# An mLSTM and RG-LRU trunk: the order of the row mask and the score weights, and the PSUM tile of a head's last chunk

## The chip, the cores and the metric

The kernel runs on one core of a Trainium2 chip. The metric is the device time of one execution in microseconds; the median of a few executions is compared. A profile is one further execution, with its own time. Engines go by their short names in the profile: PE is TensorE (matmuls), PEld its weight loads, DVE is VectorE, ACT is ScalarE, POOL is GpSimd, SP is SyncE, which here only issues DMAs.

## The reference

A two-layer decoder trunk over 2048 tokens of width 1024 in float32: an mLSTM layer, then an RG-LRU layer, each behind an RMSNorm and with a residual, and a final RMSNorm. The change concerns the middle of the mLSTM layer. Per head (4 heads, key width 256, value width 512) and chunk of tokens it computes

```python
D = F[..., :, None] - F[..., None, :] + ib[..., None, :]
D = jnp.where(causal, D, -jnp.inf)
m_t = jnp.maximum(F + m[..., None], jnp.max(D, axis=-1))
W = jnp.exp(D - m_t[..., None])
Sm = jnp.einsum('bhtk,bhsk->bhts', qb, kb) * W
num = decay[..., None] * (q C) + (Sm v);  den = decay * (q n) + sum(Sm)
hb = num / jnp.maximum(jnp.abs(den), jnp.exp(-m_t))[..., None]
C_new = d_last * C + (w_last k)^T v
```

(the einsums of `num` and `C_new` are shortened). Then `hh = o * hb` is normed over the head's 512 values to `(hh - mu) * rsqrt(var + EPS)`, scaled by `norm_w`, and `y = (hn + skip * xc) * silu(z)` goes to the output projection.

## The kernel before, in words

There are four phases: the input projections and the gate scans (a1), the mLSTM recurrence (`phase_a2`), the output projection with the second layer's input projection (b1), and the RG-LRU itself with its output (b2). Large products are split in a high and a low float32r part, three matmuls for one (lines 391 to 393); `split_into` (lines 806 and 809) makes the parts: ScalarE casts the high one, VectorE subtracts for the low one.

`phase_a2` works on 4 heads of 8 blocks, a block being 256 tokens or two chunks of 128, so a head has chunks `ch` 0 to 15. It is a software pipeline: in the loop step of block i stand block i's recurrence and block i+1's projections. In the order of the program, one step holds:

- `norm` of block i-1 (line 1144): ScalarE turns the gated `hh` to its norm with the scale and bias in `frs`.
- `loads` of block i+1: SP loads `qb` (line 918, the stabilizer of each token, broadcast over partitions), `db`, `xc`, `xm`, `sz`, `o`; the input splits `xch`, `xcl`, `xmh`, `xml`.
- `recur` of the block's first chunk: the state update `kv` (then line 1090 on VectorE, and the state's parts `Ch` and `Cl`), and the numerator `n` (scores times values, and query times the old state). Lines 1112 to 1122 divide `n` and gate it to `hh`; lines 1131 and 1132 take its mean and variance `mv`.
- `finish` of block i-1: TensorE transposes `hh` to `pt` (line 1157), ScalarE takes it out as `y` (line 1161), VectorE adds and multiplies (1163, 1164), GpSimd stores it (1166).
- `qk` of block i+1: GpSimd masks `qb` with an affine select (line 968: tokens behind the row's own get 3.0e38, so that their weight becomes 0), ScalarE makes the row weights `wgt = exp(gT - qb)` in two halves (line 974), TensorE the query and key projections, taken out as `qT` (995) and `kT` (1005); skip terms `skx`.
- `recur` of the second chunk; at its end GpSimd makes the block's `frs` in four small instructions (lines 1137 to 1140), the second of which in program order is the power -0.5.
- `score` (line 1026; VectorE multiplies by `wgt` at 1028; transposed keys `kh`, `kl`), then the value projections, taken out as `vh` and `vl`.

Besides, parts of the next head's q and k weights and of the second layer's weights are loaded, split and stored in between (`wraw`; 768 wide for the gate weights, 1024 wide for the rest), and in a head's first block the value weights `vwh`, `vwl`.

Each engine runs its instructions in a fixed order, set at build time: a scheduler goes through the program by priority and a cost model, and puts an instruction where its operands and buffers are ready by that model. `self.order(first, then)` adds a constraint: on one engine, `then` stands behind `first`; it makes no wait on another engine. Buffers are rings: `qb` and `wgt` have two each, so the mask of block j can only be loaded when the weights of block j-2 are made. PSUM has eight banks: four for tag "r" (projections, scores, transposes), two for one `kv` tile (pool `pk`), two for one `n` tile (pool `p1`). The profile's line numbers are those of this listing.

Of the kernel before, what the change touches and what calls it, by code (L numbers as in the profile page):

```python
# [7 lines left out]
F32 = mybir.dt.float32  # L8
# [6 lines left out]
P = 128  # L15
# [322 lines left out]
class Trunk:  # L338
# [481 lines left out]
    def phase_a2(self, wq, wk, wv, rgate, rwout, D, late):  # L820
# [3 lines left out]
        with ExitStack() as ctx:  # L824
# [9 lines left out]
            pk = ctx.enter_context(tc.tile_pool(name="psK", bufs=1, space=PSUM, reuse_waits="tile"))  # L834
            p1 = ctx.enter_context(tc.tile_pool(name="psS", bufs=1, space=PSUM, reuse_waits="tile"))
# [10 lines left out]
            nc.gpsimd.memset(mh, -0.5)  # L846
            halves = lambda t: t.rearrange("p (a b) -> p a b", a=2)[:, :, 0:256]
            VA = (slice(0, 258), slice(258, 516))
            self.ygated = ()
            W = {}  # L850

            def head_weights(h, names):
# [54 lines left out]
            def project(h, b):  # L907
# [58 lines left out]
                def qk():  # L966
                    qb = S["qb"]
                    selected = nc.gpsimd.affine_select(qb, qb, pattern=[[0, 2], [1, P]], compare_op=ALU.is_ge, fill=3.0e38,
                                                       base=0, channel_multiplier=-1)
                    if h and b == 1:  # L970
                        self.order(self.rooted, (selected,))
                    wgt = lx.tile([P, 2, P], F32, tag="wgt", name="wgt")
                    for c in range(2):
                        a = nc.scalar.activation(wgt[:, c], qb[:, c], AF.Exp, bias=self.gT[:, r0 + c:r0 + c + 1],
                                                 scale=-1.0)
                        if (h, b) == (0, 1):
                            self.order((self.kT,), (a,))
                        if (h, b) == (0, 2):
                            self.order(self.valued, (a,))
                        if (h, b) == (0, 0):  # L980
                            self.order(self.tail[-1:], (a,))
                            self.first = S.setdefault("w", ()) + (a,)
                            S["w"] = self.first
                    S["wgt"] = wgt
                    xh, xl = S["xc"]
                    for nm in ("q", "k"):
                        wh, wl = W[h][nm]
                        ps = pr.tile([P, 2, BL], F32, tag="r", name="pj")
                        for m in range(2):
                            for k in range(KV):  # L990
                                ms = slice(m * P, (m + 1) * P)
                                self.mm3(ps[:, m], wh[:, k, ms], wl[:, k, ms], xh[:, k], xl[:, k], k == 0, k == KV - 1)
                        t = lx.tile([P, 2, BL], F32, tag=nm + "T", name=nm + "T")
                        if nm == "q":
                            self.qT = nc.scalar.activation(t, ps, AF.Copy, scale=DK ** -0.5)
                            qd = sp.tile([P, 2, BL], F32, tag="qd", name="qd", bufs=2)
                            nc.vector.scalar_tensor_tensor(qd, ps, DK ** -0.5,
                                                           S["db"].unsqueeze(1).to_broadcast([P, 2, BL]),
                                                           op0=ALU.mult, op1=ALU.mult)
                            qh = dp.tile([P, 2, BL], F32R, tag="qh", name="qh")  # L1000
                            ql = dp.tile([P, 2, BL], F32R, tag="ql", name="ql")
                            self.qsplit = self.split_into(qh, ql, qd, "a", "v")
                            S["qd"] = (qh, ql)
                        else:
                            self.kT = nc.scalar.copy(t, ps)
                            if (h, b) == (0, 0):
                                self.order((self.kT,), self.first + self.qsplit)
                        S[nm + "T"] = t
                    if b == 0:
                        head_weights(h, ("v0", "v1"))  # L1010
                    end = (h, b) == final
                    S["skx"] = skx = (late if end else lp).tile([P, KV, BL], F32, tag="kwh" if end else "skx", name="skx")
                    for k in range(KV):
                        a = nc.scalar.activation(skx[:, k], S["xcf"][:, k], AF.Copy, scale=self.v("sk", h * KV + k))
                        if (h, b) != (0, 0):
                            self.order(self.state[:1], (a,))
                        else:
                            self.skips = (self.skips if k else ()) + (a,)
# [27 lines left out]
                def value(c):  # L1046
# [11 lines left out]
                    if (h, b, c) == (0, 0, 1):  # L1058
                        self.order(self.valued, self.skips)

                return S, [loads, qk, score, lambda: value(0), lambda: value(1)]

            C = {}

            def recur(h, b, c, S):
                ch = b * 2 + c
# [1 line left out]
                cs = slice(c * P, (c + 1) * P)  # L1068
                i = ch % NVA
                sh, sl = (t[:, c] for t in S["sm"])  # L1070
                pn = p1.tile([P, 2, 512], F32, tag="n", name="n")
                outs = tuple(pn[:, a, 0:258] for a in range(2))

                def within():
# [101 lines left out]
            for i, (h, b) in enumerate(blocks):  # L1176
                if i + 1 < len(blocks):
                    Sn, (loads, qk, score, v0, v1) = project(*blocks[i + 1])
                else:
                    Sn, loads = None, lambda: None  # L1180
                    qk = score = v0 = v1 = loads
                if last:
                    norm(*last)
                loads()
                extra = b < 5 if h == H - 1 else 2 <= b <= 6
                if extra:
                    next(later, None)
                recur(h, b, 0, S)
                if last:
                    finish(*last)  # L1190
                qk()
                recur(h, b, 1, S)
                score()
                v0()
                if extra and b == 6:
                    next(later, None)
                v1()
                if extra and b < 6:
                    next(later, None)
                if b < 2 and h < H - 1:  # L1200
                    head_weights(h + 1, "qk"[b])
                last = (h, b, S)
                S = Sn
# [746 lines left out]
```

## Time and profile before

Three executions took 2874.71, 2876.73 and 2876.86 us, a median of 2876.73. The profiled execution took 2875.3 us.

| what | value |
|---|---|
| profiled execution's own time | 2875.3 us |
| its span, first to last instruction | 2873.5 us |
| mean granted TensorE clock | 0.996 |
| TensorE busy, 0 to 1000 us (a1 and the start of a2) | 973.4 us |
| TensorE busy, 1000 to 1678.8 us (a2) | 653.7 of 678.8 us |
| TensorE busy, 1678.8 us to the end (b1, b2) | 1177.7 of 1194.7 us |
| VectorE, ScalarE, GpSimd busy in a2 | 571.6, 446.0, 120.5 us |
| DMA share of the 16 engines in a2 | 0.59 |

How to read it. A row of the waits gives engine and line, what ended the wait, the total in us, how many times, and the longest. A row of the busy times by stretch gives the stretch, its length, then PE, PEld, DVE, ACT and POOL busy with the number of instructions, the granted clock, the DMA share and GB/s. A row of the timeline gives start, length, engine, line, operation, names and shapes, and in brackets the engine's idle time before it with what ended it. Instructions of one engine overlap a little, so an idle stretch is counted from the modelled end of the one before.

### The profile page before, as it was taken

The page shows a single profiled execution, that of the slowest core. Times are in us where ns is not written, and L with a number is a line of the kernel's source. Part 1 is how long each engine was busy: PE and PEld are TensorE (multiplying, and loading weights), DVE is VectorE, ACT ScalarE, POOL GpSimd, SP SyncE. Part 2 cuts the span into 40 slices and gives each one's busy share as a digit, 9 for nine tenths or more (in the row PEclk, how much of TensorE's full clock was granted, in tenths as well). Part 3 has the DMA queues.
Part 4 walks back from the last instruction along what each step waited for, and adds up shares of the span by engine and source line. Part 5 has one row for each costly group of instructions (what it writes and reads, how often), then busy time and mean ns, then how long its engine had stood idle before and what let it go on. Part 6 is the DMA issues. An engine that isn't in the chain of part 4 may idle for free.

```text
span 2873.5 us, 43332 instructions
## 1 busy us (share of the span) xinstructions
PE 2804.8 (98%) x15442; PEld 2427.9 (84%) x15442; DVE 2132.4 (74%) x3657; ACT 1515.8 (53%) x2577; POOL 456.1 (16%) x846
## 2 busy tenths in 40 slices
PE   7999999999999999999999999999999999999998
PEld 5799987889987899998989988888788888788886
DVE  7766789635668688888888876768989658777774
ACT  6444455523444466666666653434444423977771
POOL 1211123101212211112121121101221111000000
PEclk9999999999999999999999999999999999999999
DMA  6766777668998755556575568876776765898866
GB/s 233 271 216 225 244 250 267 205 211 268 319 314 271 260 185 192 191 180 206 166 229 192 196 250 274 307 234 209 260 253 224 241 203 178 308 317 306 290 221 205
DMA packets 292472, 687.38 MB, mean 239 GB/s; under 512 B 29088, under 2 KB 103584, under 8 KB 292256
## 3 DMA queue, kind: packets, MB, share of 16 engines
q1 hardware_dynamic: 225072, 451.13, 49.1%
q0 software_dynamic: 66608, 232.43, 21.3%
q8 instruction: 122, 2.00, 0.3%
q10 hardware_dynamic: 576, 1.05, 0.1%
q14 instruction: 94, 0.77, 0.1%
HBM read 447.32 MB, written 237.17 MB: 238 GB/s over the span
## 4 chain that ended last, share of the span: by engine, by line
PE 41%; issue 4%; DVE 3%; ACT 2%; DMA 1%; POOL 1%; POOLq 0%; DVEq 0%; ACTq 0%; SPq 0%
PE pc L391 2%; PE pc L393 2%; PE pc L392 2%; PE pd L392 2%; PE pd L393 2%; PE pd L391 2%; PE pa L391 2%; PE acc L392 2%; PE pa L393 2%; PE acc L393 2%; PE pa L392 2%; PE acc L391 2%; PE pj L391 1%; PE pj L392 1%; PE pj L393 1%
## 5 line engine op out<-in xcount | busy, mean ns | idle before, releaser
L806 ACT CAST s<-raw 128x512 fp32r<-128x512 f32 (+1 forms) x280 | 172.6, 620 | 259.5 <-PE pd L393 72.7
L809 DVE TENSOR_TENSOR s<-raw,s 128x512 fp32r<-128x512 f32 (+1 forms) x280 | 192.1, 689 | 54.1 <-ACT s L806 53.1
L391 PE MATMUL acc<-yh,wr 128*128 128x512 f32 x384 | 148.5, 391 | 2.4 <-ACT R L1671 1.1
L392 PE MATMUL acc<-yl,wr 128*128 128x512 f32 x384 | 149.9, 390 | 0.2 <-DVE yl L809 0.2
L393 PE MATMUL acc<-yh,wr 128*128 128x512 f32 x384 | 149.4, 389 | 0.0
L806 ACT CAST u<-t 128x512 fp32r<-128x512 f32 x112 | 69.1, 620 | 151.8 <-PE pc L393 49.4
L732 DVE SCALAR_TENSOR_TENSOR xc<-xm,vec,xc 128x512 f32<-128x512 f32 x192 | 139.4, 747 | 5.6 <-ACT xc L731 4.9
L809 DVE TENSOR_TENSOR u<-t,u 128x512 fp32r<-128x512 f32 x112 | 77.1, 689 | 76.3 <-ACT u L806 76.3
L806 ACT CAST s<-sum 128x512 fp32r<-128x512 f32 (+1 forms) x120 | 74.1, 618 | 110.2 <-PE pc L393 39.2
L391 PE MATMUL pa<-u,s 128*128 128x512 f32 x304 | 119.1, 392 | 0.3 <-ACT y L1161 0.3
L393 PE MATMUL pa<-u,s 128*128 128x512 f32 x304 | 118.6, 390 | 0.0
L392 PE MATMUL pa<-u,s 128*128 128x512 f32 x304 | 118.5, 390 | 0.0
L1090 DVE SCALAR_TENSOR_TENSOR C<-C,dl,kv 128x516 f32<-128x516 f32 x112 | 83.8, 749 | 45.0 <-PE kv L393 45.0
L732 DVE SCALAR_TENSOR_TENSOR xc<-xr,vec,xc 128x512 f32<-128x512 f32 x144 | 105.9, 747 | 8.9 <-ACT xc L731 7.8
L806 ACT CAST Ch<-C 128x516 fp32r<-128x516 f32 x120 | 72.7, 623 | 67.8 <-DVE da L1112 53.8
L391 PE MATMUL pj<-vwh,xmh 128*128 128x512 f32 x256 | 102.8, 402 | 0.0
L393 PE MATMUL pj<-vwh,xml 128*128 128x512 f32 x256 | 100.0, 391 | 0.0
L392 PE MATMUL pj<-vwl,xmh 128*128 128x512 f32 x256 | 99.8, 390 | 0.0
L809 DVE TENSOR_TENSOR s<-sum,s 128x512 fp32r<-128x512 f32 (+1 forms) x120 | 82.4, 688 | 21.4 <-ACT s L806 20.5
L1144 ACT ACTIVATE hh<-hh,frs 128x512 f32<-128x512 f32 x64 | 51.6, 814 | 88.3 <-POOL frs L1140 88.3
L391 PEld LDWEIGHTS acc<-yh,wr 128*128 128x128 f32 x384 | 71.9, 188 | 19.5 <-DMA wr<-d_ow 1.7
L391 PE MATMUL pd<-u,s 128*128 128x512 f32 x224 | 87.1, 389 | 0.0
(501 smaller groups left out, 10055.9 us busy)
## 6 DMA issues: line engine op xcount, KB each, us to landing
wr<-d_ow SPq DMA_DIRECT2D x96, 512.0 KB, 4.4
d_wx<-s POOLq DMA_DIRECT2D x64, 512.0 KB, 4.4
s<-d_wx SPq DMA_DIRECT2D x64, 512.0 KB, 4.7
s<-d_ws SPq DMA_DIRECT2D x64, 512.0 KB, 6.3
raw<-in_wxz_dram SPq DMA_DIRECT2D x124, 256.0 KB, 4.7
d_wr<-s POOLq DMA_DIRECT2D x48, 512.0 KB, 3.8
s<-d_wr SPq DMA_DIRECT2D x48, 512.0 KB, 4.5
raw<-in_rwin_dram SPq DMA_DIRECT2D x94, 256.0 KB, 4.2
```

The source lines that it names most:

```text
L391: mm(out, sh, mh, start=first, stop=False, skip_group_check=resumed)
L392: mm(out, sh, ml, start=False, stop=False, skip_group_check=resumed)
L393: mm(out, sl, mh, start=False, stop=last, skip_group_check=resumed)
L732: self.convd = [nc.vector.scalar_tensor_tensor(out, x[:, j:j + TB], self.v(wn, m * 4 + j), out, op0=ALU.mult, op1=ALU.add) for j in range( ...
L806: a = nc.scalar.copy(hi, src)
L809: b = (nc.gpsimd if lo_eng == "p" else nc.vector).tensor_tensor(lo, src, hi.bitcast(F32), op=ALU.subtract)
L1090: v = nc.vector.scalar_tensor_tensor(C2, C2, self.dl[:, r:r + 1], p2, op0=ALU.mult, op1=ALU.add)
L1144: return [nc.scalar.activation(hn, hn, AF.Identity, bias=rs[:, 1, c:c + 1], scale=rs[:, 0, c:c + 1]) for c, hn in enumerate(S["hh"])]
```

## The change

Three edits in `phase_a2`:

1. The mask of every block is ordered behind the last of the four instructions that made the latest `frs` (`self.rooted`, empty at first). Before, this held only for the second block of heads 1 to 3.
2. The two halves of a block's `wgt` are ordered behind that block's `kT` on ScalarE, from block 3 of head 0 on.
3. The numerator `n` of a head's last chunk (`ch == 15`, which has no state update) is put in the `kv` tile instead of the `n` tile.

```diff
-            self.ygated = ()
+            self.ygated = self.rooted = ()
...
-                    if h and b == 1:
-                        self.order(self.rooted, (selected,))
+                    self.order(self.rooted, (selected,))
...
+                        weighted = (weighted if c else ()) + (a,)
...
                             self.kT = nc.scalar.copy(t, ps)
+                            if h or b > 2:
+                                self.order((self.kT,), weighted)
...
-                pn = p1.tile([P, 2, 512], F32, tag="n", name="n")
+                pn = (pk if ch == 15 else p1).tile([P, 2, 512], F32, tag="kv" if ch == 15 else "n", name="n")
```

No instruction is added or taken away. Two lines are new ahead of some of the code, so that line 1137 of before is line 1139 of the change, and so on. The orders of TensorE and VectorE stay as they were but for the first block of a head; those of ScalarE, GpSimd and SP change in nearly every block.

GpSimd in a middle block of head 0, before: the mask of a block further on, the four instructions of `frs`, two stores of weights, the store of `y`.

```order
L968 AFFINE_SELECT qb<-qb 128x256
L1137 TENSOR_SCALAR frs<-mv 128x2
L1139 TENSOR_SCALAR frs<-mv 128x2
L1138 TENSOR_TENSOR frs<-frs,mh 128x2
L1140 TENSOR_TENSOR frs<-frs 128x2
L904 DMA d_gw<-wraw 128x768 x2
L1166 DMA d_y<-y 128x4x256
```

The same place in the change:

```order
L1139 TENSOR_SCALAR frs<-mv 128x2
L1141 TENSOR_SCALAR frs<-mv 128x2
L1140 TENSOR_TENSOR frs<-frs,mh 128x2
L1142 TENSOR_TENSOR frs<-frs 128x2
L968 AFFINE_SELECT qb<-qb 128x256
L904 DMA d_gw<-wraw 128x768 x2
L1168 DMA d_y<-y 128x4x256
```

The mask went from the front of the powers to behind them. Before, 18 blocks had a mask directly in front and others none, since the masks ran up to five blocks ahead; in the change there is one behind each block's powers: behind those of block j stands the mask of block j+2.

ScalarE from `kT` on, in a middle block of head 1, before:

```order
L1005 COPY kT<-pj 128x512
L806 CAST xch<-xc 128x1024
L806 CAST Ch_12502<-C_12369 128x516
L806 CAST Ch_12526<-C_12388 128x516
L806 CAST sh<-sm 128x256
L1041 ACTIVATE kh<-kt,wlT 128x256
L974 ACTIVATE wgt<-qb,gT 128x128 x2
L1055 CAST vh_9962<-pj 128x2x256
L1041 ACTIVATE kh<-kt,wlT 128x256
L1144 ACTIVATE hh<-hh,frs 128x512
```

and in the change:

```order
L1005 COPY kT<-pj 128x512
L973 ACTIVATE wgt<-qb,gT 128x128 x2
L806 CAST xch<-xc 128x1024
L806 CAST Ch_12502<-C_12369 128x516
L806 CAST Ch_12526<-C_12388 128x516
L806 CAST sh<-sm 128x256
L1043 ACTIVATE kh<-kt,wlT 128x256
L1057 CAST vh_9962<-pj 128x2x256
L1043 ACTIVATE kh<-kt,wlT 128x256
L1146 ACTIVATE hh<-hh,frs 128x512
```

The two halves of `wgt` went from behind the first `kh` to behind `kT`. They are also those of another block now: of the block whose `kT` stands there.

VectorE at the start of head 2, from the query's low part on, before:

```order
L809 TENSOR_TENSOR ql<-qd,qh 128x512
L809 TENSOR_TENSOR vwl<-wraw,vwh 128x1024 x2
L1112 TENSOR_SCALAR da<-n 128x1
L1028 TENSOR_TENSOR sm<-s,wgt 128x256
L1113 SCALAR_TENSOR_TENSOR da<-n,da,enT 128x1
L1042 SCALAR_TENSOR_TENSOR kl<-kt,wlT,kh 128x256
L1115 RECIPROCAL da<-da 128x1
L809 TENSOR_TENSOR sl<-sm,sh 128x256
L1122 SCALAR_TENSOR_TENSOR hh<-n,da,o 128x512
L1042 SCALAR_TENSOR_TENSOR kl<-kt,wlT,kh 128x256
L1131 BN_STATS st<-hh 128x6
L1056 TENSOR_TENSOR vl_9964<-pj,vh_9960 128x2x256
```

and in the change:

```order
L809 TENSOR_TENSOR ql<-qd,qh 128x512
L1114 TENSOR_SCALAR da<-n 128x1
L1115 SCALAR_TENSOR_TENSOR da<-n,da,enT 128x1
L809 TENSOR_TENSOR vwl<-wraw,vwh 128x1024 x2
L1117 RECIPROCAL da<-da 128x1
L1030 TENSOR_TENSOR sm<-s,wgt 128x256
L1124 SCALAR_TENSOR_TENSOR hh<-n,da,o 128x512
L809 TENSOR_TENSOR sl<-sm,sh 128x256
L1133 BN_STATS st<-hh 128x6
L1044 SCALAR_TENSOR_TENSOR kl<-kt,wlT,kh 128x256
L1134 BN_AGGR mv<-st 128x2
L1058 TENSOR_TENSOR vl_9964<-pj,vh_9960 128x2x256
```

The last chunk's division went ahead of the value weights' split, and its gate and variance ahead of both `kl` and the `vl`. TensorE's order there differs by one matmul: the first product of the second value projection stands one place behind the first product of the first.

## The prediction

> **What bounds the kernel now.** I read the page's busy times first, then the waits of the mLSTM stage (985 to 1690 us), then its busy times by stretch, then two of its blocks instruction by instruction.
>
> ```profile
> PE 2804.8 (98%) x15442; PEld 2427.9 (84%) x15442; DVE 2132.4 (74%) x3657; ACT 1515.8 (53%) x2577; POOL 456.1 (16%) x846
> ```
>
> TensorE is the bound. Only what ends an idle stretch of TensorE can give time back, and only what makes one can cost any. The waits of this stage by engine:
>
> ```profile
> PE pt L1157 <- ACT hh L1144: 22.7, 24, 1.7
> ACT hh L1144 <- POOL frs L1140: 87.9, 31, 4.1
> POOL qb L968 <- DMA qb<-d_q: 140.8, 24, 9.9
> POOL frs L1137 <- DVE mv L1132: 63.4, 10, 9.4
> ```
>
> One chain stands out. TensorE's transposes `pt` wait for the normed `hh` (24 times, 22.7 us; all its other waits here are under 1 us each), ScalarE's norm waits for the powers `frs` (31 times), and GpSimd, which makes them, sits 24 times at the row mask `qb` until that mask's load lands. Only 10 times do the powers wait for what they really need, the variance `mv`.
>
> Next the busy times by stretch. Each stretch runs from the first score product (line 1026) of one block to that of another; (h, b) is head and block, from 0. The first two columns are the stretch and its length, then TensorE.
>
> ```profile
> 1040.76:1106.33 65.57, 62.70 (x459) 59.03 (x458) 54.98 (x100) 41.81 (x81) 9.98 (x23) 1.00 0.55 172
> 1106.33:1126.98 20.65, 20.65 (x155) 19.67 (x153) 18.29 (x34) 13.79 (x27) 3.23 (x8) 1.00 0.63 202
> 1126.98:1148.69 21.71, 20.90 (x154) 19.67 (x153) 18.31 (x34) 13.80 (x27) 3.68 (x9) 1.00 0.56 184
> 1148.69:1167.92 19.23, 19.23 (x143) 18.24 (x141) 17.30 (x33) 13.09 (x25) 4.57 (x8) 1.00 0.75 243
> 1188.39:1275.54 87.15, 83.52 (x611) 78.72 (x610) 73.41 (x133) 56.16 (x108) 12.28 (x29) 1.00 0.51 164
> 1296.19:1318.61 22.42, 20.88 (x154) 19.67 (x153) 18.35 (x34) 14.24 (x27) 4.04 (x9) 1.00 0.63 204
> 1318.61:1341.38 22.77, 21.15 (x142) 19.79 (x141) 17.71 (x32) 13.26 (x25) 5.97 (x8) 0.93 0.67 226
> 1341.38:1362.10 20.72, 19.68 (x143) 18.33 (x141) 17.66 (x32) 14.98 (x30) 4.38 (x7) 1.00 0.58 190
> 1362.10:1450.08 87.98, 83.56 (x611) 78.69 (x609) 73.61 (x134) 56.93 (x108) 13.42 (x29) 1.00 0.56 172
> 1450.08:1470.83 20.75, 20.75 (x154) 19.65 (x153) 18.35 (x34) 14.23 (x27) 3.61 (x8) 1.00 0.68 214
> 1470.83:1492.65 21.82, 20.91 (x154) 19.69 (x153) 18.36 (x34) 14.23 (x27) 4.01 (x9) 1.00 0.68 224
> 1536.19:1601.22 65.03, 62.62 (x458) 59.02 (x457) 55.05 (x100) 42.72 (x81) 11.88 (x25) 1.00 0.62 204
> ```
>
> Block (0,5), the second row, takes 20.65 us with TensorE busy throughout; (2,5), 1450.08, takes 20.75. The rows of their neighbours come to 21.7 to 22.4 a block. What differs is seen in (0,4), with the mask, and (0,5), without it, by variance, GpSimd, norm and transpose:
>
> ```profile
> 1089.80 0.17 DVE L1132 BATCH_NORM_AGGREGATE mv<-st 128x2 f32<-128x6 f32 x1
> 1091.35 0.41 POOL L968 TENSOR_SCALAR_AFFINE_SELECT qb<-qb 128x256 f32<-128x256 f32 x1 [6.76 <-DMA qb<-d_q]
> 1091.85 0.19 POOL L1137 TENSOR_SCALAR frs<-mv 128x2 f32<-128x2 f32 x1
> 1096.14 0.99 PE L1157 MATMUL pt<-ident,hh 128*128 128x128 f32 x7 [1.43 <-ACT hh L1144]
> ...
> 1112.12 0.17 DVE L1132 BATCH_NORM_AGGREGATE mv<-st 128x2 f32<-128x6 f32 x1
> 1112.39 0.19 POOL L1137 TENSOR_SCALAR frs<-mv 128x2 f32<-128x2 f32 x1 [5.48 <-DVE mv L1132]
> 1113.65 0.20 POOL L1140 TENSOR_TENSOR frs<-frs 128x2 f32<-128x2 f32 x1
> 1115.81 0.81 ACT L1144 ACTIVATE hh<-hh,frs 128x512 f32<-128x512 f32 x1
> 1116.75 1.04 PE L1157 MATMUL pt<-ident,hh 128*128 128x128 f32 x8
> ```
>
> Without the mask the powers start 0.27 us after `mv` starts, with it 2.05 us after: 1.78 us late, and TensorE stands 1.43 us.
>
> **Part 1, the mask behind the powers.** The mask is neither added nor dropped; by the order listing each one now follows the powers and none precedes them. So the 17 blocks that have it in front, the rows of (0,2)-(0,4), (0,6), (1,1)-(1,4), (1,6), (2,1)-(2,4), (2,6), (3,1)-(3,3), should fall to the time of those without. Against 20.65 us each that is 3.62 + 1.06 + 4.55 + 1.77 + 5.38 + 1.17 + 3.08 = 20.63 us. In 12 of the 17 a 1024-wide weight split shares the norm's place on ScalarE, as in (2,5) at 20.75: minus 12 x 0.10 = 1.2. It leaves **19.4 us**.
>
> What waits for the mask is its row weights alone. The mask of block 6 now follows the powers at 1112.39 and is over about 1114.3 (1113.65 + 0.20 + 0.41); its weights come behind the next block's kT, at about 1124.5 (1103.43 + 0.58 below, one period of 20.5 on). Ten us of slack hide it. Its load is issued behind earlier weights, two blocks ahead; on SP's queue it now stands between xc and sz, and the weights that free its buffer are over at 1104.7 (kT's end below plus their 0.68), before sz can go at 1105.62, so nothing is held there.
>
> **Part 2, the weights behind kT.** ScalarE, VectorE and the SP queue in block (0,5):
>
> ```profile
> 1103.43 0.58 ACT L1005 COPY kT<-pj 128x512 f32<-128x512 f32 x1
> 1104.86 0.62 ACT L806 CAST Ch<-C 128x516 fp32r<-128x516 f32 x1
> 1105.62 0.36 SPq L943 DMA_DIRECT2D sz<-d_sz  x1
> 1106.12 0.69 DVE L809 TENSOR_TENSOR Cl<-C,Ch 128x516 fp32r<-128x516 f32 x1
> 1107.56 0.63 ACT L806 CAST Ch<-C 128x516 fp32r<-128x516 f32 x1 [2.07 <-DVE da L1112]
> 1108.76 0.68 ACT L974 ACTIVATE wgt<-qb,gT 128x128 f32<-128x128 f32 x2
> ```
>
> The pair costs 0.68 us wherever it stands. It leaves a place ahead of an idle stretch and enters one whose next idle stretch is 2.07 us. Queued behind it are the cast xch and the first Ch. Ch then ends at 1106.16, not 1105.48; with the 0.10 us that a hand-over takes (`mv` over at 1112.29, powers at 1112.39) Cl starts at 1106.26, not 1106.12, so all that VectorE does after it, up to `mv`, comes 0.14 us later. In a narrow block TensorE has 0.13 us to spare (`hh` is over at 1116.62, `pt` starts at 1116.75), which swallows it. In the wide ones, 12 plus (2,5), (3,4), (3,5), it has none: 15 x 0.14 = **2.1 us lost**. Bounds: nothing, if VectorE takes it up, and 0.68 us in each of 24 blocks less 0.13 in nine, 15 us, if nothing does. I stay near the low end, since the 2.07 us row is three times the pair.
>
> **Part 3, the last chunk's PSUM tile, and the head boundaries.** The products are the same; what moves is which reads they wait for. VectorE and GpSimd at the start of head 2, and TensorE at the stage's end:
>
> ```profile
> 1341.48 2.36 DVE L809 TENSOR_TENSOR vwl<-wraw,vwh 128x1024 fp32r<-128x1024 f32 x2 [0.25 <-ACT vwh L806]
> 1347.32 0.17 DVE L1132 BATCH_NORM_AGGREGATE mv<-st 128x2 f32<-128x6 f32 x1
> 1347.40 1.19 DVE L809 TENSOR_TENSOR xcl<-xc,xch 128x1024 fp32r<-128x1024 f32 x1
> 1347.59 1.06 POOL L1137 TENSOR_SCALAR frs<-mv 128x2 f32<-128x2 f32 x1 [9.38 <-DVE mv L1132]
> 1350.83 0.44 PE L1157 MATMUL pt<-ident,hh 128*128 128x128 f32 x2 [1.02 <-ACT hh L1144]
> ...
> 1676.58 0.36 PE L391 MATMUL n<-vh,sh 128*128 128x258 f32 x1 [0.92 <-DVE hh L1122]
> 1680.00 0.50 PE L391 MATMUL pa<-u,s 128*128 128x512 f32 x1 [0.32 <-ACT y L1161]
> 1330.00:1335.00 5.00, 4.62 (x27) 4.60 (x27) 3.31 (x5) 3.17 (x7) 0.00 (x0) 0.66 0.68 246
> ```
>
> At a boundary VectorE's new order takes `mv` ahead of a kl and a vl split, 1.1 us by their length, but ScalarE's pair now delays the casts vwh, and with them vwl and the value product behind it, by up to 0.68. The power at 1347.59 took 1.06 us beside xcl, against 0.19 at 1112.39. With `mv` earlier it starts ahead of xcl, but the pow behind it then meets xcl. The block takes 20.72 us against 19.23 for (0,7), which has the same products: at most 1.5 us a boundary, three times, to be had; at worst 0.7 each lost to vwl. I take 0.5 each, **1.5 us**.
>
> At the end the 0.92 us wait of `n` for the previous `hh` goes, since the tile it now takes was read a step earlier. But `pa` behind it waits until 1680.00 for ScalarE's `y`, whose order of work there is nearly the same: the wait moves to `pa`. I take nothing (bounds 0 and 1.1).
>
> Blocks (1,7) (1318.61) and (2,7) lose 3.5 us each against (0,7); no mask stands in them and no edit touches what is late there. Part of it is TensorE's clock: 0.66 granted from 1330 to 1335, 1.7 us. I leave both as they are. The Trainium skill (TensorE: Matmul & The Clock Gate, part 1) has the clock halve only after an idle window of about 3.4 us; here it fell behind waits of 1.24 and 0.38 us, so the trace goes by less idle time than the page.
>
> **The sum.** 19.4 - 2.1 + 1.5 = 18.8 us off. The profiled execution took 2875.3 us, 1.8 more than its span of 2873.5, and 1.4 less than the median of the runs, 2876.73. Its span should become 2854.7, its own time 2856.5, and the median **2857.9 us**. The 600 us behind this stage shift as a whole: by the table ahead TensorE is busy there for nearly all the time, and its loads are issued as buffers come free, not at fixed times.
>
> **The rivals.**
> - *The pair's 0.68 us goes through.* Ch, Cl and `mv` all come later and TensorE waits at `pt` again, by up to 15 us in all instead of 2.1: 2857.9 + 13 = 2871. For it: Ch feeds a chain that ends in `mv`. Against: the idle 2.07 us.
> - *GpSimd meets VectorE.* Powers that start 1.8 us earlier may run beside a split such as xcl and take 0.8 us longer (1.06 against 0.19): 17 x 0.8 = 13.6 us given back, 2871. Against it: in (0,5) they stand at that very place and take 0.19. The Trainium skill (GPSIMD Engine Reference, Specifications) says that GpSimd shares its SBUF interfaces with VectorE and contends with instructions of two SBUF inputs; by that rule, with which the 1.06 us beside xcl agrees, the powers are safe beside PSUM reads and not beside splits.
> - *More comes.* The boundaries give all 4.5, the pair costs nothing and the low clock in two blocks goes: 18.8 + 3.0 + 2.1 + 3.4 = 27.3 us, 2849.
> - *Slower: the mask is late.* If it were released behind kT instead of 10 us ahead, ScalarE would stand at the weights with xch, Ch, sh and kh queued behind it, and TensorE for the last three. From about 10.2 us of lateness each further us costs one in each of the 29 blocks that have it; held one block longer (20.6 us) it would be 10 us a block, 290 us, 3167. It decides only if powers or load slip by half a block. Against: the order listing.
> - *Nothing.* The norm is late for another reason too: 2877. Against: (0,5) and (2,5).
>
> **How the numbers follow.** Forecast 2853 to 2863: 0.68. More: 0.10. Pair goes through: 0.12. Meeting VectorE: 0.03. Nothing: 0.03. Slower: 0.04. The range 2848 to 2869 takes in the forecast, nearly all of "more" and most of what lies between it and 2871. A measurement here tells about 0.2%, 5.75 us, so faster means under 2871.0: 0.68 + 0.10 + 0.08 + 0.02 = 0.88; same 0.04 + 0.01 + 0.03 = 0.08; slower 0.04.
>
> **What would show it.** GpSimd's idle time before the mask should no longer end with its load; `frs` should wait for `mv` some 30 times; TensorE's wait at `pt` should fall from 22.7 to about 6 us, left in (1,7), (2,7) and the boundaries; blocks should take 20.65 to 20.9 us. If it stays above 12 us with `mv` later against the score product, the pair goes through; if a power row reads near 1 us in plain blocks, it is VectorE. The forecast is wrong if plain blocks stay above 21.2 us.

## The result, and the profile after

The changed kernel takes 2855.79 us (median of six runs, 2851.93 to 2860.05) beside 2876.8 us of the kernel before on the same chip (six runs, 2874.13 to 2877.86): a ratio of 0.9931, 95% interval 0.9921 to 0.9941. On another chip it came to 0.9925 (0.9911 to 0.9938). The profiled execution took 2854.54 us with a span of 2852.8 us, 20.7 us less than before; forecast were 18.8 us off the span and a median of 2857.9 us.

The busy times of the changed kernel, from its page:

```profile
PE 2802.1 (98%) x15442; PEld 2427.4 (85%) x15442; DVE 2131.6 (75%) x3657; ACT 1515.6 (53%) x2577; POOL 453.3 (16%) x846
```

Every engine runs as many instructions as before, and the busy times are within 3 us of before. What went is idle time. The waits of the mLSTM stage (985 to 1670 us; engine, line, what it waited for, then us in all, times and the longest):

```profile
POOL frs L1139 <- DVE mv L1134: 173.4, 28, 21.5
ACT hh L1146 <- POOL frs L1142: 62.8, 31, 2.2
POOL qb L968 <- DMA qb<-d_q: 4.8, 2, 2.7
PE pt L1159 <- ACT hh L1146: 4.4, 7, 1.3
```

GpSimd stood 24 times, 140.8 us, for the mask's load; now twice, 4.8 us. The powers `frs` now wait for the variance `mv`, 28 times and not 10. The norm's wait for the powers fell by 25.1 us, TensorE's wait at the transposes `pt` from 22.7 to 4.4 us. The busy times by stretch, cut at the first score product of blocks (stretch, its length, then busy time of TensorE, its weight loads, VectorE, ScalarE and GpSimd, granted clock, DMA share, GB/s):

```profile
1041.11:1103.21 62.10, 62.10 (x458) 59.05 (x457) 54.95 (x100) 41.80 (x81) 9.84 (x23) 1.00 0.56 181
1103.21:1123.87 20.66, 20.66 (x155) 19.67 (x154) 18.30 (x34) 13.79 (x27) 3.62 (x9) 1.00 0.58 196
1183.82:1266.64 82.82, 82.82 (x610) 78.73 (x609) 73.28 (x133) 56.03 (x108) 12.39 (x29) 1.00 0.55 171
1308.06:1330.86 22.80, 21.18 (x142) 19.82 (x141) 17.35 (x32) 13.15 (x26) 6.35 (x9) 0.93 0.67 228
1330.86:1351.05 20.19, 19.81 (x142) 18.21 (x141) 18.14 (x33) 15.29 (x28) 2.27 (x5) 1.00 0.64 195
1434.07:1454.83 20.76, 20.76 (x155) 19.66 (x154) 18.34 (x34) 14.22 (x27) 3.98 (x9) 1.00 0.64 217
```

TensorE is now busy from end to end of (0,2)-(0,4) (first row: 62.10 us, before 65.57) and of (1,1)-(1,4) (third: 82.82, before 87.15). (0,5) (second) and (2,5) (last) stood clear of the mask already and took what they took before: 20.66 and 20.76. The boundary block (2,0) fell from 20.72 to 20.19; (1,7) still takes 22.80. Block (0,4) of the changed kernel, by the rows that the prediction showed of the kernel before:

```profile
1088.32 0.17 DVE L1134 BATCH_NORM_AGGREGATE mv<-st 128x2 f32<-128x6 f32 x1
1088.59 0.19 POOL L1139 TENSOR_SCALAR frs<-mv 128x2 f32<-128x2 f32 x1 [5.47 <-DVE mv L1134]
1090.01 0.42 POOL L968 TENSOR_SCALAR_AFFINE_SELECT qb<-qb 128x256 f32<-128x256 f32 x1
1092.97 1.03 PE L1159 MATMUL pt<-ident,hh 128*128 128x128 f32 x8
```

The powers start 0.27 us after `mv` starts (before: 2.05), the mask follows them, and the wait of 1.43 us in front of `pt` is gone.

Cut at the same places, the blocks of the stage add up as follows in the profiled runs. "Plain" are the 23 blocks of numbers 1 to 6 of a head, without (0,1); "boundary" are (1,0), (2,0), (3,0); "last" are (0,7), (1,7), (2,7). The last column is the median of the timed runs as a ratio to the kernel before on the same chip, with its interval.

| kernel | plain, us | boundary | last | ratio |
|---|---|---|---|---|
| before | 495.9 | 61.9 | 64.8 | 1 |
| changed | 476.7 | 60.4 | 64.9 | 0.9931 (0.9921-0.9941) |
| part 1 alone | 476.8 | 62.2 | 64.9 | 0.9929 (0.9914-0.9943) |
| part 2 alone | 479.3 | 67.0 | 63.3 | 0.9952 (0.9936-0.9968) |
| part 3 alone | 497.6 | 61.9 | 63.3 | 1.0001 (0.9991-1.0010) |
| parts 1 and 2 | 476.7 | 60.4 | 63.3 | 0.9926 (0.9911-0.9941) |
| two copies more ahead of Ch | 479.8 | 60.4 | 63.3 | 0.9925 (0.9910-0.9940) |
| pair and four copies behind Ch | 477.4 | 60.5 | 61.7 | 0.9920 (0.9905-0.9935) |
| split behind second value product | 476.8 | 62.3 | 57.9 | 0.9910 (0.9894-0.9927) |
| store alone behind the powers | 476.7 | 63.2 | 58.4 | 0.9918 (0.9904-0.9933) |

### The profile page after: what moved, and what is told of

It reads as the page before. It is cut to its first block, busy times and chain, and to the rows that moved or that the text cites. A ratio compares the mean times of both kernels' runs of the same rounds, so it can differ in the third digit from the quotient of the medians.

```text
span 2852.8 us, 43314 instructions
## 1 busy us (share of the span) xinstructions
PE 2802.1 (98%) x15442; PEld 2427.4 (85%) x15442; DVE 2131.6 (75%) x3657; ACT 1515.6 (53%) x2577; POOL 453.3 (16%) x846
## 4 chain that ended last, share of the span: by engine, by line
PE 80%; issue 8%; DVE 5%; ACT 2%; DMA 2%; POOL 2%; POOLq 0%; DVEq 0%; SPq 0%; ACTq 0%
PE pc L391 4%; PE pc L392 4%; PE pc L393 4%; PE pd L391 4%; PE pd L392 4%; PE pd L393 4%; PE pa L391 4%; PE pj L392 4%; PE pj L391 4%; PE pa L393 4%; PE pj L393 4%; PE pa L392 4%; PE acc L392 2%; PE acc L393 2%; PE acc L391 2%
## 5 line engine op out<-in xcount | busy, mean ns | idle before, releaser
L391 PEld LDWEIGHTS acc<-yh,wr 128*128 128x128 f32 x384 | 71.9, 188 | 19.1 <-ACT R L1673 1.6
L391 PE MATMUL pd<-u,s 128*128 128x512 f32 x224 | 87.3, 390 | 0.0
L392 PE MATMUL pd<-u,s 128*128 128x512 f32 x224 | 87.2, 389 | 0.0
```

The lines of the kernel that those rows point to most:

```text
L391: mm(out, sh, mh, start=first, stop=False, skip_group_check=resumed)
L392: mm(out, sh, ml, start=False, stop=False, skip_group_check=resumed)
```

## The experiments: which part gave it

**Part 1 alone:** the first hunk of the diff and the one that drops the condition on the mask.

```diff
-            self.ygated = ()
+            self.ygated = self.rooted = ()
-                    if h and b == 1:
-                        self.order(self.rooted, (selected,))
+                    self.order(self.rooted, (selected,))
```

> Part 1 alone: every row mask is ordered behind the norm's powers; the score weights may go where the planner puts them (here between the two Ch casts and the y copies), and the last chunk keeps its PSUM tile. Theory (what cost TensorE its time was the wait for the mask's load in front of the powers): the 17 blocks fall to 20.65 to 20.8 us, the head boundaries stay at 20.5 to 20.7, so about 1.5 us above the full change: 2857 us. Rival (the weights' new place is needed for it, since otherwise ScalarE meets the mask too early): some blocks keep 0.3 us or more, 2862 or above.

Measured: ratio 0.9929, 2856.63 us. The plain blocks take all that they take in the full change (476.8 against 476.7 us), the boundaries nothing. The theory holds; the weights' new place is not needed for the mask's gain.

**Part 2 alone:** the two additions around `weighted`.

```diff
+                        weighted = (weighted if c else ()) + (a,)
...
+                            if h or b > 2:
+                                self.order((self.kT,), weighted)
```

> Part 2 alone: the pair of score weights stands behind kT, but the masks keep their place in front of the powers, in 25 blocks. By the order of work the mask's buffer is now free, and its load issued, a good block before the mask. Theory (the wait for the load, not the place in front): GpSimd is idle before mv, so a mask whose load has landed costs nothing there; blocks 20.65 to 20.8 us, time as in the first part alone, 2857 us. Rival (the place in front is what costs, whatever the load): 25 blocks lose at least the mask's 0.41 us, and the time is between 2867 and 2877.

Measured: ratio 0.9952, 2863.72 us, between the two. My reading of the order was wrong in one point: the masks do not run a block after their load, they moved forward with it, and still wait for it 27 times, 99.2 us. But in plain blocks the load now lands about 3 us after the score product, 3 us ahead of `mv`. VectorE and GpSimd in block (2,4) of this run, by start and duration, then `sl` in (2,4) of the changed kernel, where the mask stands elsewhere:

```profile
1422.55 0.69 DVE L809 TENSOR_TENSOR Cl<-C,Ch 128x516 fp32r<-128x516 f32 x1
1423.02 0.49 POOL L968 TENSOR_SCALAR_AFFINE_SELECT qb<-qb 128x256 f32<-128x256 f32 x1 [2.62 <-DMA qb<-d_q]
1423.23 0.56 DVE L809 TENSOR_TENSOR sl<-sm,sh 128x256 fp32r<-128x256 f32 x1
```

```profile
1416.70 0.40 DVE L809 TENSOR_TENSOR sl<-sm,sh 128x256 fp32r<-128x256 f32 x1
```

The powers no longer wait for the load there, but the mask now stands in VectorE's way: the split `sl` takes 0.56 us beside it and not 0.40, the block's eight transposes `pt` later stretch over 1.27 us and not 1.12, and most of these blocks take 20.9 us, not 20.75 (479.3 against 476.7 us in all). At two boundaries the old wait is back, seen at (1,0):

```profile
1169.25 0.17 DVE L1135 BATCH_NORM_AGGREGATE mv<-st 128x2 f32<-128x6 f32 x1
1171.26 0.56 POOL L968 TENSOR_SCALAR_AFFINE_SELECT qb<-qb 128x256 f32<-128x256 f32 x1 [8.78 <-DMA qb<-d_q]
1171.91 0.19 POOL L1140 TENSOR_SCALAR frs<-mv 128x2 f32<-128x2 f32 x1
1174.28 0.33 PE L1160 MATMUL pt<-ident,hh 128*128 128x128 f32 x1 [1.66 <-ACT hh L1147]
```

`mv` is there, the mask waits 2 us longer for its load, TensorE waits, and the block takes 23.3 us against 20.0. So it was the load in front of the powers that cost; a place in front whose load lands ahead of `mv` costs only the 0.1 to 0.2 us for which the two engines meet.

**Part 3 alone, and the change without it:**

```diff
-                pn = p1.tile([P, 2, 512], F32, tag="n", name="n")
+                pn = (pk if ch == 15 else p1).tile([P, 2, 512], F32, tag="kv" if ch == 15 else "n", name="n")
```

> Part 3 alone: only the last chunk's PSUM tile is changed, masks and weights stay as before. Theory: the three head boundaries give 0.5 us each and the end of the stage nothing, 2875.3 us. Rival (the boundary gain in the full change came from the weights behind kT, not from the tile): 2876.8, boundary blocks still 20.5 to 20.7 us.

> Parts 1 and 2 together, without the last chunk's tile. Theory: the full change less the boundaries' 1.5 us, 2857.3 us, with boundary blocks back at 20.5 to 20.7 us and the 0.92 us wait of n for hh back at the end of the stage. Rival (the weights behind kT gave the boundary gain): 2855.8, boundaries at 20.0 to 20.2 us.

Measured: with the tile alone 2877.38 us, ratio 1.0001 (0.9991 to 1.0010); the change without it 2855.28 us, ratio 0.9926. Both times the rival holds. The boundary's 1.5 us come with the weights behind kT, not with the tile. Norm and powers at the start of head 2, first with part 1 alone, then with parts 1 and 2:

```profile
1337.36 0.17 DVE L1131 BATCH_NORM_AGGREGATE mv<-st 128x2 f32<-128x6 f32 x1
1337.45 1.19 DVE L809 TENSOR_TENSOR xcl<-xc,xch 128x1024 fp32r<-128x1024 f32 x1
1337.63 1.06 POOL L1136 TENSOR_SCALAR frs<-mv 128x2 f32<-128x2 f32 x1 [9.38 <-DVE mv L1131]
1340.88 0.44 PE L1156 MATMUL pt<-ident,hh 128*128 128x128 f32 x2 [1.05 <-ACT hh L1143]
```

```profile
1335.88 0.17 DVE L1134 BATCH_NORM_AGGREGATE mv<-st 128x2 f32<-128x6 f32 x1
1336.15 0.19 POOL L1139 TENSOR_SCALAR frs<-mv 128x2 f32<-128x2 f32 x1 [7.27 <-DVE mv L1134]
1336.95 1.21 DVE L809 TENSOR_TENSOR xcl<-xc,xch 128x1024 fp32r<-128x1024 f32 x1
1337.43 0.79 POOL L1142 TENSOR_TENSOR frs<-frs 128x2 f32<-128x2 f32 x1
```

The pair behind kT made the planner put `mv` ahead of a kl and a vl split, and the powers now start ahead of xcl: the third (1336.62, its usual 0.73 us) has begun before xcl, and only the last is held by it, 0.79 us and not 0.19. At the end of the stage the tile moved a wait and saved none: with it `n` no longer waits 0.92 us for `hh`, and `pa` waits 0.80 us (with the tile alone 1.07 in two waits) for `y`, where it waited 0.32.

## The experiments: what the weight pair costs

The forecast charged the pair behind kT 2.1 us. The table shows nothing of it: 476.7 us with it against 476.8 without. Two more copies of its size were put ahead of Ch, on a tile that nothing reads; the order of work of the other engines stayed word for word the same.

```diff
+            pad = late.tile([P, 128], F32, name="pad")
...
                             if h or b > 2:
+                                for _ in range(2 if b else 0):
+                                    weighted += (nc.scalar.activation(pad, self.ident[:, 0:128], AF.Copy),)
                                 self.order((self.kT,), weighted)
```

> The changed kernel with two more ScalarE copies of 128x128 behind kT (one behind the weights, one behind xch; both ahead of the first Ch) in 26 blocks: about 0.6 us more ahead of Ch; the other engines keep their order of work, and the copies go to a tile that nothing reads. Theory (the pair cost nothing because Cl was waiting behind ql on VectorE anyway; in (0,5) of the changed kernel Ch is over 0.19 us before Cl starts, so 0.1 us of room is left; behind Cl VectorE is busy without a break until mv): Cl and mv come 0.5 us later and TensorE waits for it in each, 26 x 0.4 to 0.5 = 10 to 13 us, 2866 to 2869 us. Rival (ScalarE's idle stretch of 1.6 us behind the first Ch takes it up): 2856 us.

In the second run the pair itself and four copies stand behind the first Ch:

```diff
...
+                            self.weighted = ()
                             if h or b > 2:
                                 self.order((self.kT,), weighted)
+                                for _ in range(4 if b else 0):
+                                    weighted += (nc.scalar.activation(pad, self.ident, AF.Copy),)
+                                self.weighted = weighted
...
                     self.state = self.split_into(Ch, Cl, Cm, "a", "v")
+                    if c == 1 and m == 0:
+                        self.order(self.state[:1], self.weighted)
```

> The changed kernel with the pair of weights one step later, behind the first Ch, and four such copies behind it in 26 blocks: 1.8 us in all, twice what the run with two copies adds, but in ScalarE's idle stretch behind the first Ch (1.6 us with the pair ahead of Ch, 2.1 to 2.4 without). Theory (only what stands ahead of the first Ch counts): within 2 us of the changed kernel, 2855 to 2858 us. Rival (ScalarE's added work counts wherever it stands): 26 x 1.2 = 31 us, 2887 us.

Measured: 2856.58 us (ratio 0.9925) and 2855.84 us (0.9920), neither to be told from the changed kernel by its time. For the first run that is the time of its rival. The blocks tell more: two copies ahead of Ch cost 3.1 us in the plain blocks, six operations behind it 0.7 us. So the place counts, as the theory said, but its price was about a quarter of the 10 to 13 us that I gave it. ScalarE and VectorE in (0,5) of the changed kernel, in (0,5) of before (the row that the prediction lacked), and in (0,4) with the two copies:

```profile
1100.17 0.58 ACT L1005 COPY kT<-pj 128x512 f32<-128x512 f32 x1
1100.65 0.69 ACT L973 ACTIVATE wgt<-qb,gT 128x128 f32<-128x128 f32 x2
1101.25 1.04 ACT L806 CAST xch<-xc 128x1024 fp32r<-128x1024 f32 x1
1102.18 0.62 ACT L806 CAST Ch<-C 128x516 fp32r<-128x516 f32 x1
1102.40 0.68 DVE L809 TENSOR_TENSOR ql<-qd,qh 128x512 fp32r<-128x512 f32 x1
1103.00 0.69 DVE L809 TENSOR_TENSOR Cl<-C,Ch 128x516 fp32r<-128x516 f32 x1
```

```profile
1105.51 0.68 DVE L809 TENSOR_TENSOR ql<-qd,qh 128x512 fp32r<-128x512 f32 x1
```

```profile
1085.77 0.31 ACT L1011 ACTIVATE pad<-ident 128x128 f32<-128x128 f32 x1
1085.98 0.61 ACT L806 CAST Ch<-C 128x516 fp32r<-128x516 f32 x1
1086.62 0.69 DVE L809 TENSOR_TENSOR Cl<-C,Ch 128x516 fp32r<-128x516 f32 x1 [0.24 <-ACT Ch L806]
1086.51:1107.39 20.88, 20.88 (x154) 19.65 (x153) 18.39 (x33) 14.14 (x30) 3.62 (x9) 1.00 0.62 197
```

Before and after, Cl starts 0.21 us ahead of the score product (1106.12 against 1106.33; 1103.00 against 1103.21), because both times it follows ql on VectorE. The pair holds xch back by 0.60 us (1100.65 to 1101.25), less than its length of 0.69; kT itself comes 0.14 us sooner against the score product than in before; so Ch ends 0.44 us later, and 0.20 us of room is left. A copy costs 0.21 us more (1085.77 to 1085.98). With two of them Cl does wait for Ch, 0.24 us, and the block (last row, from the view by stretch) takes 20.88 us instead of 20.68: what VectorE waited was not taken up, which speaks against the rival's idle stretch. In heads 2 and 3, where Ch ended 0.37 us ahead of Cl, most blocks lose 0.05 to 0.08 us.

## The experiments: the two blocks that stayed long

(1,7) and (2,7) kept their 3.5 us. GpSimd, VectorE and TensorE in (1,7) of the changed kernel:

```profile
1314.02 0.17 DVE L1134 BATCH_NORM_AGGREGATE mv<-st 128x2 f32<-128x6 f32 x1
1314.18 0.71 POOL L904 DMA_DIRECT2D d_ow<-wraw  x1 [5.55 <-ACT wraw L806]
1314.69 1.22 DVE L809 TENSOR_TENSOR wraw<-wraw 128x1024 fp32r<-128x1024 f32 x1
1314.96 0.99 POOL L1139 TENSOR_SCALAR frs<-mv 128x2 f32<-128x2 f32 x1
1315.97 1.23 DVE L809 TENSOR_TENSOR xml<-xm,xmh 128x1024 fp32r<-128x1024 f32 x1
1316.04 1.24 POOL L1141 TENSOR_SCALAR frs<-mv 128x2 f32<-128x2 f32 x1
1319.15 0.33 PE L1159 MATMUL pt<-ident,hh 128*128 128x128 f32 x1 [1.24 <-ACT hh L1146]
```

A store of second-layer weights stands in front of the powers (0.71 us) and pushes the first two into VectorE's splits, where they take 0.99 and 1.24 us instead of 0.19 and 0.23. Two runs take this apart: one moves the whole split behind the second value product, one only its stores behind the powers.

```diff
                 v0()
-                if extra and b == 6:
-                    next(later, None)
                 v1()
-                if extra and b < 6:
+                if extra:
                     next(later, None)
```

> The changed kernel with the second-layer weights of block 6 of a head split behind its second value product, as in blocks 2 to 5, and no longer between the two. Then no weight store stands in front of the powers on GpSimd and no 1024-wide weight split runs beside them on VectorE. Theory (these two make the norm 2.7 us late in (1,7) and (2,7), and the TensorE clock of 0.66 follows from the waits they cause): both blocks fall from 22.8 to about 19.3 us, the clock stays at 1.00, 7 us off, 2849 us. Rival (the blocks are long for what comes behind, the next head's value weights, which are loaded later still): 2856 us or above.

```diff
+            self.six = False
...
-                    for t, k in zip((hi, raw), keep):
-                        nc.gpsimd.dma_start(k, t if n == 768 else t.rearrange("p (h n) -> p h n", h=2))
+                    st = tuple(nc.gpsimd.dma_start(k, t if n == 768 else t.rearrange("p (h n) -> p h n", h=2))
+                               for t, k in zip((hi, raw), keep))
+                    if self.six:
+                        self.order(self.rooted, st)
...
                 v0()
+                self.six = b == 6
```

> The changed kernel with only the weight stores of block 6 ordered behind the powers on GpSimd; the 1024-wide split stays between the two value products on VectorE. Theory (the store's place holds the first power back by 0.7 us, and so into the split; without it the first two powers run ahead of the split in 0.2 us each and only the pow beside it is stretched, to about 1.3 us): the norm is about 1.2 us late instead of 2.7, TensorE's wait there falls below 0.5 us and the low clock goes, 5 us off, 2851 us. Rival (the split on VectorE alone makes the powers long): powers stay at 1.0 us and more, at most 1.4 us off, 2854.5 us.

Measured: 2852.41 us, ratio 0.9910 (0.9894 to 0.9927), and 2854.92 us, ratio 0.9918 (0.9904 to 0.9933). Blocks (1,7) and (2,0) of the first, then of the second, by stretch:

```profile
1307.71:1327.04 19.33, 19.33 (x143) 18.23 (x141) 16.88 (x31) 12.84 (x25) 4.56 (x9) 1.00 0.68 232
1327.04:1348.22 21.18, 20.19 (x142) 18.24 (x141) 18.54 (x33) 15.82 (x29) 2.26 (x5) 1.00 0.70 221
```

```profile
1310.76:1330.30 19.54, 19.42 (x142) 18.22 (x141) 16.86 (x31) 12.08 (x25) 5.60 (x9) 1.00 0.70 234
1330.30:1351.37 21.07, 20.09 (x143) 18.26 (x142) 18.41 (x33) 16.16 (x29) 2.30 (x6) 1.00 0.66 218
```

The cause is shown: (1,7) and (2,7) both fall to 19.33 us with the whole split moved, and to 19.55 with the store alone moved, so the store was the first cause and the splits stretched what it had delayed. With the store alone moved, the first two powers take 0.19 and 0.23 us again and only the third is held by the split, 1.73 us. But 1.8 us of 7.0 (2.8 of 6.5 in the second run) come back in the boundary blocks, where TensorE then waits up to 0.5 us a product for `vwl`, the low half of the next head's value weights. Neither forecast had this loss: the first time lies between its theory and its rival, the second at its rival's number, though its blocks bear out the theory. Block (1,0) has 0.3 us of the loss in the first run and 1.0 in the second, though (0,7) ahead of it takes 19.2 to 19.3 us in both as in the changed kernel. So the moved stores cost something of themselves there; by what path is open. The first run has the lowest ratio of all. Its interval overlaps that of the changed kernel, so that it is faster rests on its trace, whose span of 2848.5 us is 4.3 us under that of the changed kernel; it was the fastest of that run's four executions.

Three more runs tried to keep what was lost. One takes the block-6 weights out of heads 1 and 2 and gives them to blocks 5 and 6 of the last head:

```diff
-                extra = b < 5 if h == H - 1 else 2 <= b <= 6
+                extra = b < 7 if h == H - 1 else 2 <= b <= (5 if h else 6)
```

> The changed kernel with the second-layer weights of block 6 of heads 1 and 2 taken out of there and into blocks 5 and 6 of the last head, whose blocks had none: the count and the bytes stay the same. Theory (in the run with the split behind the second value product the 3.5 us of (1,7) and (2,7) were won and a part lost again, since the stores gave the buffers back later and the next head's value weights came late; with no store there at all the value weights can load in time): (1,7) and (2,7) at 19.3 us, the blocks behind them at 20.2 to 20.7 us, (3,5) and (3,6) at 20.75, against the changed kernel on the same chip 4 to 7 us off (the first if that one's low clock is absent in the runs compared). Rival (the last head has no room, or the next stage waits for weights that are stored later): no gain, or slower than the changed kernel.

> The changed kernel itself, beside the run above on the same chip, for a comparison of the two and for a further look at the clock in (1,7) and (2,7): 2856 us. If the low clock there belongs to the kernel's waits, both blocks read 22.8 us again; if it comes and goes, one or both read 21.2.

Measured: 2863.61 us, ratio 0.9950 (0.9937 to 0.9962), beside 2856.84 us and 0.9925 (0.9911 to 0.9938) of the changed kernel on the same chip: slower than it. TensorE's waits from 985 to 1760 us in that run:

```profile
PE pa L391 <- ACT s L806: 10.6, 1, 10.6
PE pj L392 <- DVE vwl L809: 1.5, 2, 0.8
```

The last head had no room: TensorE waited 10.6 us for the first weights of the next stage. (1,7) and (2,7) took 19.2 us. But (2,0) and (3,0) took 21.8 us (20.2 in the changed kernel), waiting for `vwl` though no store held its load: here it is its cast behind kT that is late. The other two runs drop the rule that puts those casts behind kT, one with block 1 of the first and block 5 of the last head taking the weights over (the second edit below, in that run alone), one on top of the moved split:

```diff
-                        else:
+                        elif h == 0:
                             self.order((self.kT,), a)
...
-                extra = b < 5 if h == H - 1 else 2 <= b <= 6
+                extra = (1 if h == 0 else 2 if h < H - 1 else 0) <= b <= (5 if h else 6)
```

> The changed kernel with the second-layer weights of block 6 of heads 1 and 2 moved to block 1 of the first head and block 5 of the last (one block of the last head, not two), and without the rule that the next heads' value weights are cast behind kT, so that ScalarE casts them ahead of it. Theory (with the powers on time in (1,7) and (2,7) the next block is held by the casts vwh behind kT, 0.76 us a product in the run that emptied block 6): (1,7) and (2,7) at 19.2 us and the blocks behind them at 20.0 to 20.5, 3.5 to 6 us off the changed kernel, 2850 to 2852 us, if the next stage no longer waits for its first weights, as it did for 10.6 us with two blocks of the last head loaded. Rival (one block more in the last head is enough for that wait, or vwl on VectorE ahead of hh delays the state): 2855 or above.

> The run with the block-6 split behind the second value product, and without the rule that the next heads' value weights are cast behind kT. Theory (the blocks at the head boundary are held there by vwh behind kT): (1,0), (2,0), (3,0) fall from 20.4, 21.2 and 20.7 us to about 20.1, 2850.5 us. Rival (their load comes late, since the stores of block 6 give the buffers back late, and a cast ahead of kT then waits for the load and holds kT): these blocks 21 us or more, 2853 us or above.

Measured: 2852.97 us, ratio 0.9928 (0.9912 to 0.9945; the kernel before took 2872.95 us on that chip), and 2857.85 us, 0.9946 (0.9931 to 0.9961). TensorE's largest wait from 985 to 1760 us in the one, then in the other:

```profile
PE s L1028 <- ACT kT L1005: 2.9, 2, 2.3
```

```profile
PE s L1028 <- ACT kT L1005: 5.7, 4, 2.1
```

Cast ahead of kT, the value weights hold kT, and the score product waits for it: the second run's rival, at all three boundaries. In the first run this happens at the first boundary alone, and (0,7) takes 21.6 us; (1,7) and (2,7) take 19.2 us, but the blocks behind them 21.1, where the state update `kv` waits 0.83 us for `vh` and 0.34 us for `vl`. Its time lies between its theory and its rival. No order tried gives both blocks their 19.3 us and the boundaries their 20.1; what would is open.

## Why the prediction was right, point by point

- **The bound and the chain** (mask's load, powers, norm, transposes): right. The powers wait for `mv` 28 times (some 30 forecast), the wait at `pt` is 4.4 us (about 6), blocks take 20.65 to 20.78 us (20.65 to 20.9). Part 2 alone shows the same wait come back at two boundaries with its load.
- **Part 1, 19.4 us:** the plain blocks fell by 19.2 us, by 19.1 with part 1 alone. The 0.10 us for a wide split was right too (20.75 us against 20.65). The ten us of slack were not tested; no wait for the weights showed.
- **Part 2, 2.1 us lost:** the mis-sized term. The step that failed is "Ch then ends at 1106.16": the pair costs 0.60 us there, not 0.68, and ScalarE came 0.14 us sooner, so Ch stayed ahead of the place that ql sets. Measured: nothing. The mechanism was right, and so was the warning that it could go through: two copies more, and it does, 3.1 us.
- **Part 3, 1.5 us at the boundaries, nothing at the end:** both sizes right (1.48 us; the wait at the end moved), the cause wrong, and the first size luck: 0.5 us a boundary was taken from between two bounds. I credited VectorE's new order to the tile; it comes with the weights behind kT. The pow was to meet xcl; it had begun before it and took its usual 0.73 us, and the power behind it was held. Comparing the order of all edits at once with that of before cannot tell which of them moved a row; each edit's own order can.
- **(1,7) and (2,7) unchanged:** right (22.80 and 22.86 us), with some luck: the low clock, 1.5 us a block, stayed away in 6 of 18 such blocks.
- **The sum:** plain 19.2, boundaries 1.5, and the first two blocks of the stage 0.9 us longer, at a wait of `kv` for `vh`. The last is no part of the change: those two blocks took between 40.3 and 42.0 us in the runs here (40.4 in the repeat of the changed kernel). The rest of the kernel moved by under 1 us. The span fell 1.9 us more than forecast, about the 2.1 that the pair was charged and did not cost; that the 0.9 us of those two blocks and the rest of the kernel cancelled is chance.
- **The rivals:** the pair's time going through, GpSimd meeting VectorE in plain blocks, a late mask and "nothing" did not come; of "more comes" the pair's share came. That GpSimd's powers are safe beside PSUM reads and not beside splits held for the powers that start beside a split, and not for one that has begun before it (the pow above).

## What to carry to other kernels

Before an operation is moved, look at what its old place made its neighbours wait for: here a 0.4 us mask cost 0.7 to 1.9 us a block because its load's wait stood in front of four small operations that TensorE needed. An operation that goes ahead of a cast on one engine is free only as long as the cast still ends before the other engine has reached it, so quote the row of what that engine does just before. A delay taken out of one block may have been covering the next one's: with the block-6 weights of heads 1 and 2 taken out altogether, (1,7) and (2,7) gained 7.2 us, and the two blocks behind them lost 3.2, from a wait for weights onward.

## What the runs showed of the hardware

**GpSimd waits out VectorE's split.** In (1,7) of the changed kernel the first power ends at 1315.95 and the split beside it at 1315.91; the second ends at 1317.28 and its split at 1317.20; the split takes its usual 1.22 us. With part 1 alone the power beside xcl ends at 1338.69 and xcl at 1338.64. So the small operation is not slowed in proportion, it is held until the split is over. In part 2's run it went the other way: the mask was there first, ended at 1423.51, and `sl`, begun at 1423.23, took 0.16 us more. The Trainium skill (SBUF — State Buffer, SBUF: two separate sides) says that, of a VectorE instruction with two SBUF inputs and a GpSimd instruction that reads SBUF, the one that starts first has the shared port pair for its whole instruction and the other is blocked. The powers behind a split agree. In the other direction the trace shows less than a whole instruction: in (1,1) of part 2's run xcl begins 0.05 us behind a mask of 0.40 us (1188.99 and 1188.94) and takes 1.43 us, only 0.21 more than its 1.22; and in (1,0) of the changed kernel xcl begins at 1170.03, beside a pow that runs from 1169.68 to 1170.41, and both take their usual time, 1.22 and 0.73 us.

**The low clock came and went with the same waits.** In nine profiled runs (1,7) and (2,7) have the same two waits at `pt`, 1.58 to 1.64 us in all. Of the 18 blocks 12 took 22.8 us and 6 took 21.2 to 21.3. Five us behind the waits in (1,7), by stretch, of the changed kernel and of the run with six operations behind Ch:

```profile
1319.50:1324.50 5.00, 4.65 (x27) 4.65 (x28) 3.09 (x5) 3.01 (x7) 0.00 (x0) 0.66 0.69 243
```

```profile
1319.90:1324.90 5.00, 4.66 (x40) 4.66 (x41) 3.31 (x6) 3.05 (x8) 0.00 (x0) 1.00 0.87 240
```

27 products in one, 40 in the other, at 0.66 and 1.00 of the clock, after waits of 1.24 + 0.38 and 1.20 + 0.38 us. That is 1.5 us a block, and the length of the waits does not decide it: four runs have one block of each kind. So some 3 us of the 7 that the moved split won hang on the clock in the run it is compared with. The same program was not seen in both: the changed kernel, profiled twice, took 22.8 us all four times. The Trainium skill (TensorE: Matmul & The Clock Gate, Part 1) describes a free-running activity window of about 3.4 us; that the outcome hangs on where the waits fall in such a window would fit, but no run here shows the window.
